# First FFN's down sums: copied from PSUM by ScalarE and added to the residual in DRAM by accumulating DMAs, in groups of up to four hidden tiles

## The chip, the cores and the metric

The kernel runs on one core of a Trainium2 chip. The metric is the time of one launch on the device, in microseconds (us). TensorE is called PE here, VectorE DVE, ScalarE ACT, GpSimd POOL, and SP is the engine that issues most of the DMAs.

## The reference, cut to what matters

One decoder layer on 1088 tokens (a prompt of 1024 and 8 x 8 sample tokens) of width 1024, in float32:

```python
def _swiglu(h, w_gate, w_up, w_down):
    return (jax.nn.silu(h @ w_gate) * (h @ w_up)) @ w_down
...
    x = x + 0.5 * _swiglu(_rmsnorm(x, ffn_a_norm), ffn_a_gate, ffn_a_up, ffn_a_down)
    h = _rmsnorm(x, mix_norm)
    q, k, v, u, g_attn, g_ssm = jnp.split(h @ w_in, SPLIT_POINTS, axis=-1)
...
    x = x + merged @ w_out
    x = x + 0.5 * _swiglu(_rmsnorm(x, ffn_b_norm), ffn_b_gate, ffn_b_up, ffn_b_down)
```

The change is in the product with `ffn_a_down` (hidden width 2816 = 22 tiles of 128) and its addition to `x`.

## The kernel before

Everything is held transposed: a tile has 128 channels on its partitions and up to 1088 tokens along its rows, so the residual `x` is eight tiles `xr0` to `xr7` (index `m`), and the FFN's hidden values are 22 tiles `hid0` to `hid21` (index `j`). The tokens are cut into three columns `c` of 384, 384 and 320. Float32 products are made of three matmuls each: weights and inputs are split into a high part (a rounded copy, by ACT, line 104) and a low part (the rest, by DVE, line 105), and `mm3` (line 113) multiplies high by high, high by low, and low by high.

The first FFN (phase `a`) first computes all hidden tiles and stores them in DRAM (`hd`). Then come the *down units* that the change touches, made by `d_unit`: each takes a group of two or three hidden tiles and, for each of the 24 pairs (m, c), runs 3 matmuls for each of its tiles into a PSUM tile `psda`, and line 817 on DVE adds half of the PSUM tile to `xr`. The groups are the list `cuts` in `ffn_units` (line 1885): tiles 0-1, 2-4, 5-7, 8-10, 11-13, 14-16, 17-18, 19-21. PSUM tiles come from two rings of three and two (`"ddada"`), so five are in use at most. The second FFN (phase `b`) has the same units with `psdb`.

The residual is read from DRAM (`xd`) when the first unit starts (`need_x`, line 1784) and stays in SBUF until the last unit, which goes through the columns one after the other and starts the next RMSNorm: squares on ACT, their sums over the channels by PE (line 499), a power on POOL (line 156), then the scaled tiles for the next projection (`psu`).

All tiles of this size come from one pool of 43 buffers (`NB`, tag `B`): weights, hidden tiles, their high and low parts, and `xr`. A tile that is given a used buffer waits until the one that held it is no longer read. `run_units` issues the loads of the next two groups when a unit starts. While a unit's matmuls are issued, each `yield` issues one step of the next unit's `prep` (the split of one hidden or weight tile: ACT, then DVE) and, by `tick`, one step of a *side program*. From the second unit (tile 2) on this is `ssm_setup`, which makes tables for the later state-space part: DVE operations on 128x512 tiles in 8 rounds, with two sets of PE transposes (`cT`, line 1072, and `vl`, line 1092), one set of PE matmuls (`k`, line 1100), ACT copies and sines, and stores of tables by POOL's DMAs. All instructions of an engine run in the order in which they are issued.

Of the kernel before, what the change touches and what calls it, by code (L numbers as in the profile page):

```python
# [7 lines left out]
F32 = mybir.dt.float32  # L8
F32R = mybir.dt.float32r
AF = mybir.ActivationFunctionType  # L10
OP = mybir.AluOpType
# [9 lines left out]
T = 1088  # L21
# [45 lines left out]
class Kern:  # L67
# [711 lines left out]
    def d_unit(s, ph, js, last=None):  # L779
        nc = s.nc  # L780
        stt = {}

        class U:
            st = stt

            def load(u):
                st = u.st
                for j in js:
                    r = s.B([128, D], f"rdown{ph}{j}", F32)
                    nc.sync.dma_start(r, s.a[f"ffn_{ph}_down"][0, j * 128:(j + 1) * 128, :])  # L790
                    st[j] = r
                    r = s.B([128, T], f"rhid{ph}{j}", F32)
                    nc.sync.dma_start(r, s.hd[j])
                    s.hid[j] = r
                if js[0] == 0:
                    s.need_x(0)

            def prep(u):
                st = u.st
                eng = s.nc.vector  # L800
                for j in js:
                    hi, lo = s.B([128, T], f"hidh{ph}{j}"), s.B([128, T], f"hidl{ph}{j}")
                    s.split(s.hid[j], hi, lo, eng)
                    s.hid[j] = hi, lo
                    yield
                    s.wsplit(st, j, [128, D], f"dn{ph}{j}", eng)
                    yield

            def one(u, m, c):
                st = u.st  # L810
                o, n = CH[c]
                u.n = getattr(u, "n", 0) + 1
                ps = s.bank("ddada"[u.n % 5], f"psd{ph}{js[0]}_{m}_{c}")
                yield from s.mm3(ps[:, :n], [(st[j][0][:, m * 128:(m + 1) * 128], st[j][1][:, m * 128:(m + 1) * 128],
                                              s.hid[j][0][:, o:o + n], s.hid[j][1][:, o:o + n]) for j in js])
                xs = s.need_x(m)[:, o:o + n]
                nc.vector.scalar_tensor_tensor(xs, ps[:, :n], 0.5, xs, op0=OP.mult, op1=OP.add)  # L817

            def main(u):
                if last is None:  # L820
                    order = [(0, 0), (0, 1), (1, 0), (1, 1), (0, 2), (1, 2)] + [(m, c) for m in range(2, KC) for c in range(3)]
                    for i, (m, c) in enumerate(order):
                        yield from u.one(m, c)
                        if i % 2:
                            yield
                    return
                for c in range(3):
                    for m in range(KC):
                        yield from u.one(m, c)
                        s.sq_add(c, m, last[0])  # L830
                        yield
                    s.sq_flush()
                    s.pending += s.norm_steps(c, *last)
        return U()
# [1047 lines left out]

    def ffn_units(s, ph, last):
        s.hid = {}
        cuts = (0, 2, 5, 8, 11, 14, 17, 19, 22)
        out = [s.g_stage(ph)]
        if ph == "b":
            out.insert(0, s.plain_unit(ph))
        js = [tuple(range(a, b)) for a, b in zip(cuts, cuts[1:])]
        out += [s.d_unit(ph, j) for j in js[:-1]]  # L1890
        out.append(s.d_unit(ph, js[-1], last) if last else s.last_unit(ph, js[-1]))
        return out
# [119 lines left out]
```

## Time and profile before

| | |
|---|---|
| median of 3 runs | 2351.44 us (2351.07 to 2352.85) |
| the profiled execution's own time | 2351.03 us |
| its span, from the first to the last instruction | 2349.3 us |
| PE busy | 2275.0 us (97%) |
| DVE busy | 1404.2 us (60%) |
| ACT busy | 853.0 us (36%) |
| POOL busy | 264.3 us (11%) |

The first FFN's down units run from 514.2 to about 831.8 us after the span's start, those of the second FFN from 2069.2 to about 2295 us. Shares over the whole span say little about either; the rows below are of these stretches.

### The profile page before, as it was taken

To read this page: it belongs to the slowest core of one execution; us is meant where nothing else is said; L and a number is where in the kernel's file an instruction comes from. 1 tells how busy PE (TensorE), PEld (TensorE's weight loads), DVE (VectorE), ACT (ScalarE), POOL (GpSimd) and SP (SyncE) were. 2 spreads that over 40 slices of the span, in tenths; PEclk is the share of its full clock that TensorE was granted. 3 is DMA by queue.
4 is the path that set the end of the run, shared out by engine and by line. 5 is a ranking of instruction groups with operands and counts; after the bars stand their busy time and mean duration, and the time that the engine had idled before them with its cause. 6 is when DMAs were issued, how large, how long until landed. Compare 5 with 4: busy or idle time off the path is not lost. (4 is left out here: it accounts for less than half of the span.)

```text
span 2349.3 us, 39687 instructions
## 1 busy us (share of the span) xinstructions
PE 2275.0 (97%) x15910; PEld 2216.6 (94%) x15910; DVE 1404.2 (60%) x2961; ACT 853.0 (36%) x1919; POOL 264.3 (11%) x427
## 2 busy tenths in 40 slices
PE   7999999999889999999999999999999999999998
PEld 6999999998878998999998999989999999999997
DVE  7655555568888742446775666457555555575555
ACT  5333333331221341236666653223333333322113
POOL 2000000014333140002221100000000000000000
PEclk9999999999999999999999999999999999999999
DMA  6222222273443237740224164203222222362202
GB/s 197 79 73 83 83 75 64 83 255 108 140 138 106 73 131 215 238 107 28 69 75 111 45 231 136 73 5 140 79 83 66 73 83 83 126 256 72 86 10 77
DMA packets 234104, 250.04 MB, mean 106 GB/s; under 512 B 35056, under 2 KB 197024, under 8 KB 233888
## 3 DMA queue, kind: packets, MB, share of 16 engines
q1 hardware_dynamic: 218208, 205.42, 28.2%
q0 software_dynamic: 14272, 39.79, 4.8%
q8 instruction: 125, 2.05, 0.4%
q10 hardware_dynamic: 1440, 2.31, 0.3%
q14 instruction: 59, 0.48, 0.1%
HBM read 176.93 MB, written 74.60 MB: 107 GB/s over the span
## 5 line engine op out<-in xcount | busy, mean ns | idle before, releaser
L817 DVE SCALAR_TENSOR_TENSOR xr<-psdb,xr 128x384 f32<-128x384 f32 x168 | 87.9, 534 | 93.2 <-PE psdb L113 92.9
L817 DVE SCALAR_TENSOR_TENSOR xr<-psda,xr 128x384 f32<-128x384 f32 (+1 forms) x192 | 100.7, 532 | 33.5 <-PE psda L113 33.1
L1534 POOL TENSOR_SCALAR sm<-sm,sum 128x256 f32<-128x256 f32 x128 | 59.9, 487 | 312.3 <-DVE sum L1532 202.9
L113 PE MATMUL Ya<-b21h,a12a 128*128 128x272 f32 x320 | 67.1, 290 | 0.0
L113 PE MATMUL Xa<-t4h,a22a 128*128 128x272 f32 x320 | 67.1, 290 | 0.0
L113 PE MATMUL Yb<-b21h,a12b 128*128 128x272 f32 x320 | 67.1, 290 | 0.0
L113 PE MATMUL Xb<-t4h,a22b 128*128 128x272 f32 x320 | 67.1, 290 | 0.0
L113 PE MATMUL Vb<-b22h,s4b 128*128 128x272 f32 x320 | 67.1, 290 | 0.0
L113 PE MATMUL Va<-b22h,s4a 128*128 128x272 f32 x320 | 67.1, 290 | 0.0
L732 POOL DMA_DIRECT2D hd<-hidb x40 | 21.6, 540 | 403.0 <-DVE hidb L730 403.0
L732 POOL DMA_DIRECT2D hd<-hida x40 | 21.6, 540 | 403.0 <-DVE hida L730 403.0
L1518 ACT ACTIVATE sm<-sm,nm 128x256 f32<-128x256 f32 x128 | 63.3, 503 | 2.0 <-DVE nm L1505 1.9
L113 PE MATMUL Xa<-t2h,s2a 128*128 128x272 f32 x320 | 63.8, 290 | 0.0
L113 PE MATMUL Va<-t1h,s1a 128*128 128x272 f32 x320 | 63.8, 290 | 0.0
L113 PE MATMUL Xa<-t3h,s3a 128*128 128x272 f32 x320 | 63.8, 290 | 0.0
L113 PE MATMUL Xb<-t2h,s2b 128*128 128x272 f32 x320 | 63.8, 290 | 0.0
L113 PE MATMUL Xb<-t3h,s3b 128*128 128x272 f32 x320 | 63.8, 290 | 0.0
L113 PE MATMUL Vb<-t1h,s1b 128*128 128x272 f32 x320 | 63.8, 290 | 0.0
L113 PE MATMUL Xb<-b11h,a11b 128*128 128x272 f32 x320 | 63.8, 290 | 0.0
L113 PE MATMUL Xa<-b11h,a11a 128*128 128x272 f32 x320 | 63.8, 290 | 0.0
L104 ACT ACTIVATE hidhb<-rhidb 128x1088 fp32r<-128x1088 f32 x22 | 24.3, 1103 | 89.7 <-PE psdb L113 65.1
L113 PEld LDWEIGHTS Ya<-b21h,a12a 128*128 128x128 f32 x320 | 52.7, 188 | 0.0
(1455 smaller groups left out, 8498.9 us busy)
## 6 DMA issues: line engine op xcount, KB each, us to landing
xr<-xd SPq DMA_DIRECT2D x24, 544.0 KB, 6.0
rhida<-hd SPq DMA_DIRECT2D x22, 544.0 KB, 5.2
rhidb<-hd SPq DMA_DIRECT2D x22, 544.0 KB, 5.2
rdowna<-in_ffn_a_down_dram SPq DMA_DIRECT2D x22, 512.0 KB, 3.9
rdownb<-in_ffn_b_down_dram SPq DMA_DIRECT2D x22, 512.0 KB, 4.8
hd<-hida POOLq DMA_DIRECT2D x40, 272.0 KB, 2.9
hd<-hidb POOLq DMA_DIRECT2D x40, 272.0 KB, 2.7
rgatea<-in_ffn_a_gate_dram SPq DMA_DIRECT2D x20, 512.0 KB, 3.9
```

What stands on the lines that cost most here:

```text
L104: s.nc.scalar.activation(hi, raw, AF.Copy)
L113: s.nc.tensor.matmul(ps, w, x, start=i == 0 and not more, stop=i == n - 1, skip_group_check=more)
L732: nc.gpsimd.dma_start(s.hd[j, :, o:o + HC], hid[j][:, o:o + HC])
L817: nc.vector.scalar_tensor_tensor(xs, ps[:, :n], 0.5, xs, op0=OP.mult, op1=OP.add)
L1518: A.activation(sm[:, h, :], sm[:, h, :], AF.Exp, bias=nm[:, h:h + 1], accum_out=sm4[:, h:h + 1])
L1534: s.nc.gpsimd.tensor_scalar(sm[:, h, :], sm[:, h, :], sm4[:, h:h + 1], 1.0, op0=OP.mult, op1=OP.mult)
```

## The change

In the first FFN's units but the last (`u.dram`), the residual is no longer loaded. ACT copies half of each PSUM tile into a new tile `dy` (line 821 of the changed kernel), and when a channel tile's third column is there, POOL issues a DMA that adds the `dy` tile to `xd` in DRAM (line 823). The last unit (tiles 19-21) is as before, but it is now the one that loads `xr`. The groups of phase `a` become 0-1, 2-4, 5-8, 9-12, 13-15, 16-18, 19-21: seven units instead of eight. Phase `b` keeps its groups.

```diff
         class U:
             st = stt
 
+            dram = ph == "a" and last is None
+
             def load(u):
...
-                if js[0] == 0:
+                if js[0] == 0 and not u.dram:
                     s.need_x(0)
...
+                if u.dram:
+                    if m not in u.y:
+                        u.y[m] = s.B([128, T], f"dy{js[0]}_{m}", F32)
+                    nc.scalar.activation(u.y[m][:, o:o + n], ps[:, :n], AF.Copy, scale=0.5)
+                    if c == 2:
+                        nc.gpsimd.dma_start(s.xd[m], u.y[m], accum_op=OP.add)
+                    return
                 xs = s.need_x(m)[:, o:o + n]
                 nc.vector.scalar_tensor_tensor(xs, ps[:, :n], 0.5, xs, op0=OP.mult, op1=OP.add)
 
             def main(u):
+                u.y = {}
...
-        cuts = (0, 2, 5, 8, 11, 14, 17, 19, 22)
+        cuts = (0, 2, 5, 9, 13, 16, 19, 22) if ph == "a" else (0, 2, 5, 8, 11, 14, 17, 19, 22)
```

The matmuls are the same in number, and PE's order differs only in where the side program's matmuls stand. Three places show what moves.

DVE while the unit of tile 5 runs. Before, the evictions (`xr<-psda`) stand between the splits of the next unit's tiles (`hidla`, `dna..l`) and the side program's operations (`ph`, `lo`, `kk`, `S`):

```order
L817 SCALAR_TENSOR_TENSOR xr0_5266<-psda5_0_1_6323,xr0_5266 128x384
L105 TENSOR_TENSOR hidla8_6337<-rhida8_5854,hidha8_6336 128x1088
L1132 TENSOR_TENSOR ph0_6292<-ph0_6292,kc0_6294 128x512
L1133 TENSOR_TENSOR lo0_6295<-lo0_6295,kk0_6293 128x512
L105 TENSOR_TENSOR dna8l_6352<-rdowna8_5852,dna8h_6351 128x1024
L1135 TENSOR_TENSOR ph0_6292<-ph0_6292,lo0_6295 128x512
L1136 TENSOR_SCALAR ph0_6292<-ph0_6292 128x512
L817 SCALAR_TENSOR_TENSOR xr1_5268<-psda5_1_0_6342,xr1_5268 128x384
L105 TENSOR_TENSOR hidla9_6369<-rhida9_5858,hidha9_6368 128x1088
```

In the changed kernel the same stretch of DVE holds splits and side operations alone:

```order
L105 TENSOR_TENSOR hidla9_6376<-rhida9_5858,hidha9_6375 128x1088
L1142 TENSOR_TENSOR ph0_6324<-ph0_6324,kc0_6326 128x512
L1143 TENSOR_TENSOR lo0_6327<-lo0_6327,kk0_6325 128x512
L105 TENSOR_TENSOR dna9l_6391<-rdowna9_5856,dna9h_6390 128x1024
L1145 TENSOR_TENSOR ph0_6324<-ph0_6324,lo0_6327 128x512
L1146 TENSOR_SCALAR ph0_6324<-ph0_6324 128x512
L105 TENSOR_TENSOR hidla10_6412<-rhida10_5862,hidha10_6411 128x1088
```

The evictions have left DVE; nothing else there has changed its place.

ACT in the same stretch, first before:

```order
L104 ACTIVATE dna8h_6351<-rdowna8_5852 128x1024
L104 ACTIVATE hidha9_6368<-rhida9_5858 128x1088
L1138 ACTIVATE kk0_6293<-ph0_6292 128x512
L1139 ACTIVATE kk0_6293<-kk0_6293 128x512
L1140 ACTIVATE ph0_6292<-ph0_6292,c1_68 128x512
L104 ACTIVATE dna9h_6377<-rdowna9_5856 128x1024
```

and in the changed kernel:

```order
L821 ACTIVATE dy5_1_6400<-psda5_1_0_6381 128x384
L104 ACTIVATE hidha10_6411<-rhida10_5862 128x1088
L1148 ACTIVATE kk0_6325<-ph0_6324 128x512
L1149 ACTIVATE kk0_6325<-kk0_6325 128x512
L1150 ACTIVATE ph0_6324<-ph0_6324,c1_68 128x512
L821 ACTIVATE dy5_1_6400<-psda5_1_1_6402 128x384
L104 ACTIVATE dna10h_6423<-rdowna10_5860 128x1024
```

The copies out of PSUM (line 821) now stand in ACT's queue, some of them behind the sine `kk<-ph` (line 1148; line 1138 before), which reads what DVE makes.

POOL at the end of the side program, just before the last unit. Before:

```order
L1143 DMA tab3_5555<-kk7_7869 128x4x128
L1144 DMA tab3_5555<-ph7_7868 128x4x128
L1147 DMA tab2_5554<-kpad_5556 16x32x128 x8
L156 TENSOR_TENSOR rstd_8366<-ms_8362,mhalf_79 128x3
```

and in the changed kernel:

```order
L823 DMA xd_84<-dy16_5_8102 128x1088
L1153 DMA tab3_5547<-kk7_8116 128x4x128
L1154 DMA tab3_5547<-ph7_8115 128x4x128
L823 DMA xd_84<-dy16_6_8151 128x1088
L1157 DMA tab2_5546<-kpad_5548 16x32x128 x8
L823 DMA xd_84<-dy16_7_8202 128x1088
L156 TENSOR_TENSOR rstd_8414<-ms_8410,mhalf_79 128x3
```

The last accumulating DMA, that of channel tile 7, stands behind the eight copies of `kpad` to the table, and the load of `xr7` for the last unit has to wait for it.

## Rows read from the trace of the kernel before

**Rows 1.** The page's first part: busy us (share of the span) and instructions.

```profile
span 2349.3 us, 39687 instructions
PE 2275.0 (97%) x15910; PEld 2216.6 (94%) x15910; DVE 1404.2 (60%) x2961; ACT 853.0 (36%) x1919; POOL 264.3 (11%) x427
```

**Rows 2.** Busy time by stretch: down units of phase a, then all with side program.

```profile
core 0: us, PE busy (x) PEld busy (x) DVE busy (x) ACT busy (x) POOL busy (x), PEclk, DMA share, GB/s
514.20:538.00 23.80, 23.80 (x146) 23.80 (x145) 19.09 (x31) 7.74 (x9) 16.65 (x31) 1.00 1.03 365
538.00:584.40 46.40, 41.64 (x234) 38.65 (x233) 39.62 (x132) 6.45 (x9) 15.62 (x8) 0.93 0.15 46
631.40:679.50 48.10, 42.74 (x246) 39.88 (x246) 40.68 (x73) 11.66 (x18) 18.07 (x28) 0.93 0.41 127
...
769.10:792.90 23.80, 23.80 (x146) 23.80 (x146) 18.80 (x30) 4.02 (x5) 5.85 (x10) 1.00 0.46 155
792.90:832.00 39.10, 38.06 (x236) 37.63 (x236) 30.32 (x60) 18.20 (x34) 10.44 (x10) 1.00 0.05 14
538.00:769.10 231.10, 207.81 (x1197) 195.98 (x1196) 198.07 (x415) 54.27 (x77) 80.28 (x107) 0.95 0.36 110
```

**Rows 3.** The same for three units of three tiles in phase b.

```profile
2093.00:2200.00 107.00, 107.00 (x651) 107.00 (x650) 57.90 (x90) 17.50 (x18) 0.00 (x0) 1.00 0.25 82
```

**Rows 4.** Who waited for whom, 514 to 832 us: total, times, longest.

```profile
ACT kk L1138 <- DVE ph L1136: 76.5, 7, 13.1
...
PE vl L1092 <- DVE S L1080: 12.7, 5, 5.5
...
PE psda L113 <- DVE xr L817: 7.7, 6, 2.6
...
PE k L1100 <- DVE C L1087: 2.9, 2, 2.2
```

**Rows 5.** PE by line, 537 to 832 us, the side program's matmuls: busy, mean ns.

```profile
L1100 PE MATMUL k<-C,S 128*16 128x128 f32 x64 | 10.3, 314 | 2.9 <-DVE C L1087 2.9
...
L1092 PE MATMUL vl<-c,S 128*128 128x128 f32 x32 | 6.3, 333 | 12.7 <-DVE S L1080 12.7
L1072 PE MATMUL cT<-c,ssmin 64*128 64x64 f32 x16 | 2.7, 247 | 0.0
```

**Rows 6.** DVE by line, 538 to 769 us: evictions, splits, one side operation.

```profile
L817 DVE SCALAR_TENSOR_TENSOR xr<-psda,xr 128x384 f32<-128x384 f32 (+1 forms) x120 | 63.3, 531 | 18.5 <-PE psda L113 18.3
L105 DVE TENSOR_TENSOR hidla<-rhida,hidha 128x1088 fp32r<-128x1088 f32 x14 | 18.0, 1283 | 0.0
...
L1126 DVE TENSOR_TENSOR kk<-ph,lo 128x512 f32<-128x512 f32 x8 | 5.5, 688 | 0.1
```

**Rows 7.** ACT by line, whole span: a copy of 128x384 out of PSUM.

```profile
L1403 ACT ACTIVATE ts<-pswgs 128x384 f32<-128x384 f32 x16 | 7.9, 492 | 21.9 <-PE pswgs L113 19.1 <-issue 2.8
```

**Rows 8.** DMA, 862 to 875 us, where stores of xr fill the queues.

```profile
q1 hardware_dynamic: 1972, 4.16, 91.4%
```

**Rows 9.** DMA issues on the page: KB each, us to landing.

```profile
xr<-xd SPq DMA_DIRECT2D x24, 544.0 KB, 6.0
...
hd<-hida POOLq DMA_DIRECT2D x40, 272.0 KB, 2.9
```

**Rows 10.** POOL in order of time, 768 to 776 and 514 to 600 us: start, us.

```profile
769.93 4.38 POOL L1147 DMA_DIRECT2D tab<-kpad  x7
775.07 0.64 POOL L1147 DMA_DIRECT2D tab<-kpad  x1 [0.75 <-DMA tab<-ph]
...
548.63 6.51 POOL L959 TENSOR_TENSOR prm<-prm 128x32 f32<-128x32 f32 x1 [2.21 <-DVE prm L956]
```

## Prediction, made before the changed kernel had run

> **What bounds the kernel now.** I read the first part of the page first: PE is busy in 97% of the span and no other engine in more than 60% [rows 1]. Over the whole kernel there is little to win, so the question is whether the changed stretch is one of the poor ones. The busy times by stretch say that it is [rows 2]. The unit of tiles 0-1 and that of tiles 17-18 run with PE busy throughout (23.80 of 23.80 us). Between them, from 538.0 to 769.1 us, five units of three tiles take 231.1 us; PE is busy in 207.8 of these, its granted clock is 0.95, and DVE is busy in 198.1 (86%). What differs there is the side program, whose DVE work shares the queue with the evictions.
>
> The control is phase b, where the same units run without a side program [rows 3]: three units in 107.0 us, or 35.67 each, with PE at 100%, clock 1.00, and the evictions still on DVE. Five units at that pace are 5 x 35.67 = 178.3 us, so the side program costs 231.1 - 178.3 = 52.8 us. Part of that is PE's own side work: its three groups are busy for 10.3 + 6.3 + 2.7 = 19.3 us [rows 5]. Matmuls overlap in the pipeline, so their net cost is less than that sum; half of it (about 10) is my lower end and 19.6 (the sum, rounded up) the upper; I take 15. This leaves 52.8 - 15, about 38 us (33 to 43), for waits and the loss of clock that goes with them.
>
> The waits name the places [rows 4]: PE waits 12.7 us in `vl` and 2.9 in `k` for DVE tables, and 7.7 in `psda`, where the eviction of an earlier PSUM tile (line 817) has not yet run. That is only 23.3 us of the 38; the rest I put down to matmuls at the lower clock (0.93 in the units shown) and to short gaps which that view does not group. The long waits of ACT (76.5 us in 7, for `ph` of DVE) cost nothing now, since nothing that PE needs soon stands behind them.
>
> **What goes.** In tiles 2 to 16 there are 120 evictions by DVE of 531 ns, 63.3 us in all [rows 6]. They all leave. DVE's work in this part falls from 198.1 to 134.8 us, 70% of the 193.3 us (178.3 + 15) that PE alone needs there. In the whole phase seven groups in place of eight make 168 evictions instead of 192, of which 144 are on ACT and the last unit's 24 stay on DVE.
>
> **What ACT gets.** The nearest row for a copy of 128x384 out of PSUM is 492 ns [rows 7], so the 144 copies are about 70 us (a little less, since every third is of 320). The part of tiles 2 to 16 gets some 115 of them, 56 us, on top of 54.3 [rows 2]: 110 of 193, or 57%. By load this is hidden. By order it may not be, which is a rival below.
>
> **The regrouping** changes no matmul. A group of four fills a PSUM tile in 1.98 us, one of three in 35.67 / 24 = 1.49. It costs nothing in itself; what it needs is buffers.
>
> **What POOL and the queues get.** 48 accumulating DMAs of 544 KB. Issue on POOL is bounded by its own rows: 0.64 us for one transfer of the `kpad` group, 4.38 for seven [rows 10], so 40 of them are some 25 us beside POOL's 80.3 in 231 [rows 2]; not a bound. On the queues, the stretch that is full of stores moved 4.16 MB at 91.4% of 13 us [rows 8], 11.9 us, so a plain 544 KB (0.557 MB) fills all 16 engines for 1.59 us. Tiles 2 to 18 have 40 of them: 64 us at that price. The queues' own work there is 0.36 x 231.1 + 0.46 x 23.8 = 94 us [rows 2], together 158 of some 225 us. So at the plain price the transfers are hidden.
>
> No row shows an accumulating DMA. Its lower bound is the plain 1.59 us; for the upper I go by 3 times that, 4.8 us, a read of the target and a write in place of one write with as much again lost to turning round (an estimate from that row, not a measurement). I take the plain price to twice it, in which the sum does not change: twice, 94 + 127 = 221, is just below 225.
>
> On this the Trainium skill has a rule that speaks against the change ("Collectives: The Full Stack", section "The bandwidth ceiling: the fold count and why AG ≠ RS ≠ AR"): a reducing transfer has two source reads for one write and so runs at about half the rate of a copy. No run here shows it yet. By the rule the sum would have 127 us of accumulates in place of 64, which is a rival below.
>
> **What is left of the 38 us.** Three costs stay or come.
>
> First, the bursts of DVE. At each `yield` DVE gets a split of 1.28 us and a side operation of about 0.69 [rows 6], while PE needs for the matmuls in between (eight of about 0.165 us, from 35.67 us for 216 matmuls) 1.3 us. DVE falls behind by up to some 5 to 8 us while the splits run and catches up in the other half of the unit. So PE's waits for `vl` and `k` do not all go: bounds 0 and 15.6 (12.7 + 2.9, [rows 4]); I take 6, under half, as the queue is shorter by the evictions.
>
> Second, the new `dy` tiles want used buffers, so an ACT copy may wait for an accumulate to land (in the order, the third `dy` tile of a unit takes the buffer of the second one, or of one two before). A plain store of 272 KB lands after 2.9 us and a load of 544 KB after 6.0 [rows 9]; I put an accumulate between 2.9 and 12. One `dy` tile is delayed also by the 6.51 us power on POOL, behind which its accumulate stands [rows 10]. Five PSUM tiles give PE 4 x 1.49 = 6 us to 4 x 1.98 = 7.9 us of slack. Most such waits lie within it: bounds 0 and 5, taken 2.
>
> Third, the last unit. It was PE-bound with a loaded `xr` (38.06 of 39.10, [rows 2]). Now `xr7` is loaded behind the last accumulate, and that stands on POOL behind eight copies of `kpad`, 4.38 + 0.64 = 5.0 us [rows 10]. Landing (6 to 12) and loading (6.0, [rows 9]) take 12 to 18 us. The first use of `xr7` comes eight groups later, 8 x 1.49 = 11.9 us, and PE is held only at the norm's sums that follow. Bounds 0 and 6; taken 2. The first unit, whose queues are full (1.03, [rows 2]), no longer has the eight loads of `xr`; as PE has no gap there, that gives nothing.
>
> **The sum.** 38 - 6 - 2 - 2 = 28 us. The profiled execution took 2351.03 us with a span of 2349.3, 0.4 us below the median of 2351.44, so the bases agree: 2351.0 - 28 = 2323 us. With the ends: 43 and no residual cost give 2308; 33 - 15.6 - 2 - 6 = 9 gives 2342.
>
> **The rivals.** *A, twice the price.* The 221 us of DMA would fit on average, but the side program's stores are bunched (0.15 of the queues in one unit, 0.41 in another, [rows 2]). At the density of 91.4% [rows 8] 221 us become 242, 17 more than 225; with good luck none. Half of it, 8 us: 2331 us. For it speaks that the add must read its target; against it that reads and writes may overlap.
>
> *B, ACT in PSUM's way.* The copies stand behind `kk<-ph`, for which ACT waits 76.5 us in 7 waits, 10.9 each, longest 13.1 [rows 4]. Behind these PE has 7.9 us of slack in a unit of four tiles. If DVE stays as late as now, each of eight rounds costs PE 10.9 - 7.9 = 3 us, 24 in all, and the gain is 28 - 24 = 4: 2347 us. Against it: without the evictions DVE reaches `ph` sooner, by the 63.3 us spread over eight rounds, 8 us each.
>
> *C, the other side.* The accumulates bound the stretch. They must then take so long that the queues need the whole 254.9 us (231.1 + 23.8) of before, less the 2 at the end: (252.9 - 94) / 40 = 4.0 us each, 2.5 times the plain price, or 2.2 times at a density of 91.4%. From there on ACT waits for buffers, PE for ACT, and the kernel is slower. At three times it is 94 + 191 = 285 us, 312 at that density; the middle, 299, is 44 above 254.9 and with 2 for the end gives 2397 us. For it speaks that `dy` waits chain directly into ACT's queue; against it, that a plain load of 544 KB lands in 6.0 us although many share the queues [rows 9], so that an add would have to cost far more than its read.
>
> **How the numbers follow.** Forecast .64 (its own range 2308 to 2342), A .14, B .12, C .10. The predicted time is the forecast's, 2323. The range of 8 in 10 is 2311 to 2342: it holds the forecast but for its lowest tail, and A; what is left out is C (.10), the larger part of B (.07) and tails (.03). A change of 0.2%, 4.7 us, is about what a measurement of this kernel can tell from none. Slower by more than that: C, .10. Within it: half of B, .06. Faster: the forecast, A and the other half of B, .84.
>
> **What would show it.** In the changed trace the stretch of tiles 2 to 18 should take some 225 us in place of 255, with DVE near 70%, ACT near 57% and PE's clock near 1.00. `psda` should wait for ACT in place of DVE, by a few us in all; `vl` and `k` for DVE by half of now. An accumulate's share of the queues should be near 0.7 in that stretch; if it is near 0.9 or above and ACT's longest waits are for buffers that a DMA frees, A or C is right. If ACT's waits for `ph` stay near 11 us and PE waits for the copies behind them, B is. The wait at the last unit for `xr7` should be below 6 us. I would be wrong by most if an accumulate has a latency far above 12 us, since then every reuse of a `dy` buffer stops ACT and so PE, though the queues are not full.

## The result, and the profile after

The changed kernel is slower: 2372.18 us (median of 4 runs, 2371.33 to 2373.76) against 2351.28 of the kernel before; ratio 1.0088, interval 1.0071 to 1.0106. I had forecast 2323 us, 28 us faster; it is 21 us slower, outside the range of 2311 to 2342. Of my cases, the one on the other side (C, chance .10) had the right sign, but not the right way to it.

From the page of the changed kernel, its first part, two lines of the part on DMA (queue: packets, MB, share of 16 engines) and the line of the accumulates (count, KB each, median us to landing); they answer to [rows 1, 8, 9]:

```profile
span 2370.6 us, 39777 instructions
PE 2279.5 (96%) x15910; PEld 2221.8 (94%) x15910; DVE 1329.7 (56%) x2793; ACT 913.0 (39%) x2063; POOL 308.4 (13%) x475
...
q0 software_dynamic: 21184, 66.53, 11.1%
...
HBM read 176.93 MB, written 101.34 MB: 117 GB/s over the span
...
xd<-dy POOLq DMA_DIRECT2D x48, 544.0 KB, 7.8
```

The same lines on POOL's queue in the kernel before:

```profile
q0 software_dynamic: 14272, 39.79, 4.8%
...
HBM read 176.93 MB, written 74.60 MB: 107 GB/s over the span
```

DVE lost 74.5 us of work (1404.2 to 1329.7), as it should. POOL's queue grew from 4.8% of 2349.3 us to 11.1% of 2370.6, by 263.1 - 112.8 = 150.3 us: 3.13 us of all 16 engines for each of the 48 accumulates, twice the plain 1.59 of [rows 8]. The bytes written grew by their 26.7 MB; the bytes read did not change, so if an add reads its target, this count does not show it; the share of the queues does show the longer time.

Where did the time go? The busy times by stretch, one row for each unit from tile 2 on, then the units of tiles 2 to 18 together (compare [rows 2]):

```profile
core 0: us, PE busy (x) PEld busy (x) DVE busy (x) ACT busy (x) POOL busy (x), PEclk, DMA share, GB/s
537.30:600.90 63.60, 45.19 (x234) 42.91 (x234) 33.68 (x113) 19.44 (x35) 26.93 (x20) 0.81 0.94 222
600.90:659.40 58.50, 53.16 (x317) 51.08 (x317) 32.92 (x51) 24.93 (x44) 25.99 (x37) 0.97 0.77 174
659.40:712.60 53.20, 51.94 (x318) 49.98 (x317) 28.66 (x45) 22.93 (x42) 26.23 (x37) 1.00 0.91 228
712.60:757.30 44.70, 41.40 (x237) 39.27 (x236) 31.33 (x50) 21.04 (x42) 25.50 (x36) 0.92 0.88 209
757.30:801.10 43.80, 40.59 (x241) 38.90 (x240) 26.68 (x42) 19.80 (x38) 14.64 (x19) 0.96 0.98 236
801.10:853.00 51.90, 41.07 (x237) 40.33 (x236) 30.34 (x60) 20.07 (x40) 18.79 (x22) 0.87 0.45 128
537.30:801.10 263.80, 232.28 (x1339) 222.13 (x1339) 153.26 (x300) 108.14 (x199) 119.28 (x148) 0.93 0.89 213
```

Two rows stand out: the unit of tiles 2-4 takes 63.6 us (46.4 before) and the last one 51.9 (39.1 before). In each PE is idle a long time, and its granted clock is lower (0.81 and 0.87). The middle units have queues as full (0.77 to 0.98) and lose little: a full queue alone does not stop PE here.

The waits in the unit of tiles 2-4 (total, times, longest; compare [rows 4]):

```profile
engine line waited for: us in total, times, longest us
DVE hidla L105 <- ACT dy L821: 20.7, 1, 20.7
...
PE psda L113 <- ACT dy L821: 14.8, 2, 10.2
...
ACT hidha L104 <- DMA xd<-dy: 14.5, 1, 14.5
```

PE waits for a copy by ACT, but it is not the copy that is slow: ACT itself stands for 14.5 us before the *split* of the next unit's first hidden tile (`hidha5`; the views leave numbers out), until an accumulate lands. In time, POOL first, then its eight accumulates as a group (first and last issue; shortest, median and longest time to landing), then SP, ACT and DVE (start, duration, idle time before and what ended it):

```profile
531.35 4.07 POOL L943 DMA_DIRECT2D kpad<-zero  x8 [0.29 <-POOL zero L941]
535.41 7.13 POOL L823 DMA_DIRECT2D xd<-dy  x8
539.85 8.19 POOL L960 TENSOR_TENSOR prm<-prm 128x32 f32<-128x32 f32 x1
...
L823 POOL DMA_DIRECT2D xd<-dy x8: 983/2078/3263, 535.4 to 539.3; - x8
...
DMA to landing us min/median/max: 5.6/16.7/29.9
...
511.02 0.33 SPq L795 DMA_DIRECT2D rhida<-hd  x1
541.09 0.33 SPq L792 DMA_DIRECT2D rdowna<-in_ffn_a_down_dram  x1
...
541.06 0.49 ACT L821 ACTIVATE dy<-psda 128x384 f32<-128x384 f32 x1 [1.07 <-PE psda L113]
556.10 1.11 ACT L104 ACTIVATE hidha<-rhida 128x1088 fp32r<-128x1088 f32 x1 [14.55 <-DMA xd<-dy]
...
569.25 1.06 ACT L104 ACTIVATE dna7h<-rdowna 128x1024 fp32r<-128x1024 f32 x1 [7.07 <-issue]
...
560.16 1.29 DVE L105 TENSOR_TENSOR hidla<-rhida,hidha 128x1088 fp32r<-128x1088 f32 x1 [20.70 <-ACT dy L821]
```

The first `dy` tile was full at 519 us. But POOL was issuing the side program's opening transfers (from 515.9 to 535.4 us): the side program's first step is issued ahead of the unit of tiles 0-1, only the rest runs from tile 2 on. So the eight accumulates of tiles 0-1 left together, from 535.4 to 539.3 us: 25 us of queue time (8 x 3.13) at once. They land one after the other, the first at 541.0 us (5.6 after its issue), the last at 569.2 (29.9 after). The buffers of their `dy` tiles go, by the order of the pool, to four loads of SP (the first leaves at 541.09) and to `hidha5`, `hidla5`, `hidla7` and `dna7h` of the next unit: not to other `dy` tiles, but to splits that stand at the head of ACT's and DVE's queues. The trace fits this to a tenth of a microsecond where it can be read best: the fifth, sixth and eighth accumulate land at 556.1, 560.1 and 569.2, and the splits of `hidha5`, `hidla5` and `dna7h` start at 556.10, 560.16 and 569.25. (DVE's wait is put down to a copy by ACT that had long been done, and ACT's second one, of 7.07 us, to no releaser.) Behind the held split on ACT stand the copies, and behind these the five PSUM tiles and PE. PE stands twice, for 10.6 us until 558.6 and for 4.9 us until 570.7, and both ends follow such a split.

In the last unit (POOL, then SP, then DVE, then PE's wait by the view of waits):

```profile
803.41 0.95 POOL L823 DMA_DIRECT2D xd<-dy  x1
803.98 4.09 POOL L1157 DMA_DIRECT2D tab<-kpad  x6
808.90 0.63 POOL L1157 DMA_DIRECT2D tab<-kpad  x1 [0.82 <-DMA tab<-ph]
812.24 0.63 POOL L1157 DMA_DIRECT2D tab<-kpad  x1 [2.71 <-DMA xd<-dy]
813.38 0.91 POOL L823 DMA_DIRECT2D xd<-dy  x1 [0.51 <-ACT sqtf L481]
...
822.63 0.32 SPq L1794 DMA_DIRECT2D xr<-xd  x1
...
819.50 0.56 DVE L826 SCALAR_TENSOR_TENSOR xr<-psda,xr 128x384 f32<-128x384 f32 x1 [6.29 <-DMA xr<-xd]
826.46 0.56 DVE L826 SCALAR_TENSOR_TENSOR xr<-psda,xr 128x384 f32<-128x384 f32 x1 [5.93 <-DMA xr<-xd]
...
PE sspf L499 <- DVE sqsumf L488: 9.8, 1, 9.8
```

The accumulate of channel tile 7 was issued at 813.4 us, 10 us after that of tile 6; `xr7`'s load was issued at 822.6, and DVE had it at 826.5. PE stood before the norm's sums, for 10.1 us from start to start of its matmuls (9.8 in the view of waits). About half of those 10 us between two accumulates is the issue of eight copies; the rest comes from the program as it is built. POOL's DMAs use eight semaphores in turn, and each waits until the transfer eight places before it has landed. The seventh copy of `kpad` waits so for the table's `ph`, the eighth for the accumulate of tile 6 (landed at 811.95), and the accumulate of tile 7 for the first copy (812.83).

### The profile page after: what moved, and what is told of

Same layout as the page of the kernel before. It is cut to its first block, busy times and chain, and to the rows that moved or that the text cites. A ratio compares the mean times of both kernels' runs of the same rounds, so it can differ in the third digit from the quotient of the medians.

```text
span 2370.6 us, 39777 instructions
## 1 busy us (share of the span) xinstructions
PE 2279.5 (96%) x15910; PEld 2221.8 (94%) x15910; DVE 1329.7 (56%) x2793; ACT 913.0 (39%) x2063; POOL 308.4 (13%) x475
## 3 DMA queue, kind: packets, MB, share of 16 engines
q0 software_dynamic: 21184, 66.53, 11.1%
## 5 line engine op out<-in xcount | busy, mean ns | idle before, releaser
L821 ACT ACTIVATE dy<-psda 128x384 f32<-128x384 f32 x144 | 65.6, 472 | 84.4 <-PE psda L113 75.4
L729 ACT ACTIVATE ua<-ua 128x272 f32<-128x272 f32 x40 | 17.3, 432 | 93.7 <-DVE ua L728 93.7
```

What stands on the lines that cost most here:

```text
L729: A.activation(d["u"], d["u"], AF.Silu)
L821: nc.scalar.activation(u.y[m][:, o:o + n], ps[:, :n], AF.Copy, scale=0.5)
```

## The experiments

Theory 1: an accumulate costs the queues twice a plain transfer, and that matters where something waits for one to land, at the two ends. Theory 2: the copies in ACT's queue hold PSUM, whatever the DMAs cost. Others are named where they come. Each run went beside runs of the kernel before (2352.0 to 2352.4 us). The unit lengths below, from the first `psda` matmul of a unit to that of the next (of the last unit, to the next projection), are of the profiled runs, in us; the unit of tiles 0-1 took 23.8 in all of these.

| kernel | 2-4 | 5-8 | 9-12 | 13-15 | 16-18 | 19-21 | median |
|---|---|---|---|---|---|---|---|
| changed | 63.6 | 58.5 | 53.2 | 44.7 | 43.8 | 51.7 | 2372.2 |
| plain stores | 50.0 | 56.6 | 53.2 | 43.9 | 42.5 | 45.6 | 2347.6 |
| no DMAs | 43.2 | 56.6 | 53.2 | 43.9 | 42.5 | 38.8 | 2338.5 |
| plain in the middle | 62.7 | 56.7 | 53.2 | 45.7 | 44.0 | 50.0 | 2367.1 |
| plain at the ends | 50.6 | 60.0 | 53.2 | 44.0 | 42.5 | 45.4 | 2353.1 |
| `kpad` after | 62.9 | 61.0 | 53.2 | 43.8 | 42.5 | 46.0 | 2367.1 |
| opening later | 53.2 | 64.3 | 53.2 | 43.7 | 44.1 | 47.5 | 2366.9 |
| both | 53.3 | 63.9 | 53.2 | 43.8 | 42.5 | 46.2 | 2359.7 |

**Plain stores.**

```diff
-nc.gpsimd.dma_start(s.xd[m], u.y[m], accum_op=OP.add)
+nc.gpsimd.dma_start(s.xd[m], u.y[m])
```

> The 48 DMAs write dy over the residual in DRAM instead of adding to it; the addition is left out, all else stays. Theory 1 (an accumulate takes about 3.1 us of all 16 queues, twice a plain transfer, and so frees dy buffers and xr7 too late): the time on POOL's DMA queue falls by some 70 us, the stall of the unit of tiles 2-4 (10.6 and 4.9 us) and that at the norm's sum in the last unit (10.1 us) shrink to about half, and the time is near 2355 us. Theory 2 (the copies stand in ACT's queue in the way of PSUM, whatever the DMA costs): within 4 us of the changed kernel, 2372.

Measured: 2347.55 us, ratio to before 0.9982 (0.9973 to 0.9991). Its page:

```profile
q0 software_dynamic: 21184, 66.53, 8.0%
...
xd<-dy POOLq DMA_DIRECT2D x48, 544.0 KB, 4.2
```

The same packets and bytes take 8.0% of 2344.5 us, 187.6; less 112.8 that is 1.56 us for a transfer. So the add itself costs 24.6 us of the kernel's time (2372.18 to 2347.55), more than I had expected. PE's two stops in the unit of tiles 2-4 fall from 15.5 to 2.9 us, that in the last unit from 10.1 to 4.4: theory 1.

**No DMAs.** The two lines with the DMA go.

> The 48 accumulating DMAs are left out, so the sums of tiles 0 to 18 are lost; the copies by ACT, the groups and the loads of xr in the last unit stay. Theory 1 (the transfers are what costs): both long stalls go, with the low clock behind them, and the stretch comes down to what I had forecast, 2325 to 2335 us. Theory 2 (ACT's queue): only the last unit's wait goes, 12 us, 2360 us, and PE still waits for copies in the units of tiles 5 to 18.

Measured: 2338.51 us, 0.9946 (0.9931 to 0.9961): 14 us better than before. The end of both long stalls is theory 1's, and 9.0 us of the plain stores' time goes too; but the time is not what I had forecast for free transfers. The two units of tiles 13 to 18 each still hold PE for 3.5 us before `psda`, and here theory 2 is right on a small scale. ACT and DVE in the unit of tiles 13-15:

```profile
699.48 0.45 ACT L821 ACTIVATE dy<-psda 128x320 f32<-128x320 f32 x1
706.83 0.63 ACT L1146 ACTIVATE kk<-ph 128x512 f32<-128x512 f32 x1 [6.90 <-issue]
...
708.63 0.47 ACT L821 ACTIVATE dy<-psda 128x384 f32<-128x384 f32 x1
...
706.32 0.43 DVE L1144 TENSOR_SCALAR ph<-ph 128x512 f32<-128x512 f32 x1
```

The sine waits until 706.83 us for DVE's `ph` (done 706.75), and the copies stand behind it: my rival B.

**Groups of before.** The changed kernel with the eight groups, 56 accumulates.

> The changed kernel with the eight groups of before (56 accumulates). Theory 1: eight more accumulates are 25 us more on queues that are nearly full, 2375 to 2390 us. Theory 2, in the form that the groups of four tiles leave too few free buffers: faster than the changed kernel, about 2360 us.

Measured: 2374.58 us, 1.0099 (1.0082 to 1.0116). The groups of four are not the cause of the loss as a whole: with the old ones, and eight accumulates more, the time is 2.4 us higher. They do bear on the first stall: with the old groups the unit of tiles 2-4 takes 53.9 us in place of 63.6, and the later units take that back. The new groups alone, with evictions by DVE, were not tried. By a count of tiles, two groups of four that are split (32), the raw tiles of a third (8) and `xr` (8) are more than the 43 buffers.

**Which accumulates cost?** Plain stores for the middle units, and for the first and the last before the end:

```diff
-nc.gpsimd.dma_start(s.xd[m], u.y[m], accum_op=OP.add)
+nc.gpsimd.dma_start(s.xd[m], u.y[m], **({} if js[0] in (5, 9, 13) else dict(accum_op=OP.add)))
...
+nc.gpsimd.dma_start(s.xd[m], u.y[m], **({} if js[0] in (0, 16) else dict(accum_op=OP.add)))
```

> The changed kernel with plain stores in the units of tiles 5-8, 9-12 and 13-15 (24 of 48; the addition is left out there). If the accumulates cost time at the two ends alone (what waits for the first unit's, and for the last unit's), the time stays within 5 us of the changed kernel, 2367 to 2372. If their use of the queues as a whole sets the time, half of the 24.6 us that the plain stores won come back: 2360 us.

> The changed kernel with plain stores in the units of tiles 0-1 and 16-18 (16 of 48; the addition is left out there). If the ends are what costs, nearly the whole 24.6 us come back: 2348 to 2354 us. If use of the queues sets the time, a third of it: 2364 us.

Measured: 2367.11 us (24 plain in the middle, 5 us back) and 2353.11 us (16 plain at the ends, 19 us back). Together that is 24.1 of the 24.6 of all 48; the eight accumulates of the unit of tiles 2-4 add in both runs. Use of the queues as a whole would have given 12 and 8. The ends are what costs.

**Order on POOL.** First, the eight copies of `kpad` after the last accumulate:

```diff
+for _ in range(6):
+    yield
 for r in range(8):
     nc.gpsimd.dma_start(s.tab2[:, r * 16 ...
```

> The changed kernel with the side program's last eight copies of kpad issued six steps later, so that the last accumulate stands ahead of them on POOL. If the last unit's 10.1 us wait comes from the order on POOL (the last accumulate was issued 10 us after the one before it), the wait falls to about 5 us and the time to 2366 to 2368 us. If the DMA queues are so full that the order of issue makes no difference, 2372 us.

Measured: 2367.07 us, 1.0061 (1.0044 to 1.0078), PE's stop 4.7 us. As expected of the order. Second, 17 instructions of the side program's opening later:

```diff
 load_part(0)
-load_part(1)
-z = s.sm([16, 512], "zero")
-nc.gpsimd.memset(z, 0.0)
-for q in range(8):
-    nc.gpsimd.dma_start(kpad[:, 4 * q:4 * q + 4, 0:128], z...
 yield
...
+zeros(6)
+load_part(1)
 cmul(ER, EI, ...
```

> The changed kernel with 17 POOL instructions of the side program's start (the second set of ssmin loads, the zeros and their eight copies to kpad) moved about a unit later, so that the accumulates of tiles 0-1 are issued as their dy tiles are ready, from about 519 us in place of 535. If lateness on POOL makes the stall of the unit of tiles 2-4, its 63.6 us come down to about 50 and the time to 2357 to 2362 us. If the price of eight accumulates on the queues (25 us) makes it, the unit keeps most of its length and the time is above 2367 us.

Measured: 2366.88 us (2360.77 to 2369.14; the profiled run, from which the unit lengths are, is the fastest of the four, by 5.7 us), 1.0059 (1.0044 to 1.0074), above what lateness alone should give. POOL's accumulates of tiles 0-1 in it, and the split of `dna7h` on ACT:

```profile
522.72 4.52 POOL L823 DMA_DIRECT2D xd<-dy  x5
...
L823 POOL DMA_DIRECT2D xd<-dy x8: 852/967/1932, 522.7 to 534.7; - x8
...
DMA to landing us min/median/max: 5.4/15.6/20.4
...
555.21 1.06 ACT L104 ACTIVATE dna7h<-rdowna 128x1024 fp32r<-128x1024 f32 x1 [6.11 <-issue]
```

The accumulates leave from 522.7 us on, and the unit of tiles 2-4 falls by 10.4 us, as expected of the order (to 53.2; 50 was named). The rest of its stall is the price: the eight still land one after the other, the last at 555.1 us, 20.4 after its issue; the split of `dna7h` starts at 555.21, and PE, which has stood for 6.0 us, goes on at 556.6. The next unit grows by 5.8 us. Both moves together:

> Both moves together, with all 48 accumulates. If the whole loss is order on POOL at the two ends, the gains add: 2350 to 2356 us, level with the kernel before, and above the 2338.5 of the run without DMAs by the accumulates' price alone. If the transfers are what bounds, 2365 us or more.

Measured: 2359.68 us, 1.0033 (1.002 to 1.0046). The gains add (5.1 and 5.3 alone, 12.5 together, within the spread), but to less than expected: still 7.5 us slower than before, between the two cases that were named. The eighth accumulate lands at 557.6 us and `dna7h` starts at 557.70; PE has stood for 6.4 us by then. The same pair of times, within 0.1 us of each other, stands in every run of the table that has transfers, plain stores too (553.9 and 553.98). A run that gives the `dy` tiles buffers of their own was not made. Why the unit of tiles 5-8 takes 63.9 us there instead of 58.5 was not settled; PE's waits for `vl` and `k` in it are 2 us longer and its granted clock is 0.89.

**The adds on POOL, in SBUF.** The kernel before with `xr` kept, for all columns and (with `c == 2` in the condition too) for the third alone:

```diff
+if ph == "a" and last is None:
+    y = s.t(f"ev{js[0]}_{m}_{c}")[:, :n]
+    nc.scalar.activation(y, ps[:, :n], AF.Copy, scale=0.5)
+    nc.gpsimd.tensor_tensor(xs, xs, y, op=OP.add)
+    return
 nc.vector.scalar_tensor_tensor(xs, ps[:, :n], 0.5, xs, ...
```

> The kernel before, with xr kept in SBUF and the groups of before; ACT copies half of each PSUM tile to a small tile (six of them rotate) and POOL adds it to xr there. No DMA is added. If POOL has the room (24 adds a unit of 0.7 to 1.5 us in 46 us, an estimate from its 487 ns on 128x256), the units shorten as in the run without DMAs and the time is 2335 to 2343 us. If the adds stand on POOL behind its waits for DVE (up to 12.9 us each), the six tiles run out, ACT stops and PE with it, and the time is above 2365 us.

> The same for the third column alone: 56 of the 168 evictions by ACT and POOL, the others by DVE as before. If DVE's load sets the waits of before in proportion, a third of the 14 us that the run without DMAs won, 2346 to 2348 us; if POOL's waits stop ACT, they stop it here too, but the six tiles last three times as long: 2352 or more.

Measured: 2449.34 us (1.041, 1.0394 to 1.0427) and 2369.68 us (1.0078, 1.0063 to 1.0093); both worse, the second well above the 2352 from which its worse case began. From the first, POOL by line and the waits, 514 to 940 us:

```profile
L820 POOL TENSOR_TENSOR xr<-xr,ev 128x384 f32<-128x384 f32 x168 | 182.0, 1110 | 23.0 <-ACT ev L819 22.1
...
ACT ev L819 <- POOL xr L820: 47.8, 36, 16.8
...
PE psda L113 <- ACT ev L819: 44.6, 10, 13.7
```

An add takes 1.11 us, within my bounds, and ACT does run out of small tiles. The rest is in the last section.

**Groups of four a unit later, and the sines later.** Both moves on POOL with cuts at 0, 2, 5, 8, 12, 16, 19; then two `yield`s ahead of the first sine, in place of one after each of two other steps.

> Both moves on POOL, and the groups 0-1, 2-4, 5-7, 8-11, 12-15, 16-18, 19-21: the groups of four come one unit later, so that the first unit's dy buffers are not wanted at once by four-tile loads. All 48 accumulates add. If the first loss is buffers wanted before the accumulates land, the unit of tiles 2-4 falls from 53.3 to about 48 us and the next one loses less: 2348 to 2354 us, level with the kernel before. If the groups make no difference, 2358 to 2361 us as with both moves alone.

> The same, with the side program's sines on ACT issued two steps later (two other steps are joined, so that it ends where it did). If the copies that stand on ACT behind the sine, waiting for DVE's ph, are what holds PE in psda in the units of tiles 12 to 18 (two waits of 3.5 us there), these waits go: 4 to 8 us below the run without this. If DVE's lateness only shows elsewhere (in vl and k), no difference, within 3 us.

Measured: 2363.98 us (1.0051, 1.0038 to 1.0065) and 2360.47 us (1.0039, 1.0026 to 1.0051). With the later fours, the unit of tiles 2-4 does fall to 46.9 us, but the next two (of three and of four tiles) take 57.9 and 60.6: the lateness moves on. With the sines later, the waits in question go, and others grow. PE's waits, 514 to 850 us, without and with:

```profile
PE psda L113 <- ACT dy L821: 16.3, 4, 8.8
...
PE vl L1107 <- DVE S L1095: 13.4, 3, 7.0
```

```profile
PE vl L1106 <- DVE S L1094: 24.7, 4, 13.2
PE psda L113 <- ACT dy L821: 4.4, 2, 4.0
```

The 16.3 us before `psda` fall to 4.4, and `vl` waits 11.3 us more. The units of tiles 2 to 18 together lose 2.8 us (261.7 to 264.5 in the profiles), and what is gained is in the last unit (39.9 in place of 46.8), where `xr7` has landed 16.3 us after the unit's start in place of 20.7. So one wait goes and another comes. How much of it is DVE's own lateness is not shown: in the longest wait of `vl` (13.2 us) DVE itself stands for 5.07 us before the split of `hidla10`, whose buffer is that of a `dy` tile which lands just then. No version here beats the kernel before with the sums intact.

## Why the prediction was wrong

The starts of PE's matmuls split the stretch of tiles 2 to 18 into parts, in us. The 1224 matmuls of `psda` at their median distance (174 ns for 384 columns, 147 for 320) make 202.0 in each kernel; a distance over 0.6 us counts as a wait, and the extra time of shorter ones as low clock where less than 0.9 of it was granted. The line between waits and low clock is good to about 1 us.

| kernel | stretch | side work | waits in `psda` | waits in `vl`, `k`, `cT` | low clock | short gaps |
|---|---|---|---|---|---|---|
| before | 254.8 | 16.1 | 9.4 | 17.0 | 6.2 | 4.2 |
| no DMAs | 239.4 | 14.0 | 6.7 | 9.3 | 3.3 | 4.1 |
| changed | 263.9 | 14.8 | 22.9 | 11.4 | 9.1 | 3.7 |

**What bounds it** was right: side work 16 us (I took 15), everything else 36.8 (38). (The 115 copies that I put in tiles 2 to 16 are 104 by the groups; nothing rests on them.)

**The price of an accumulate** was within my bounds (1.59 to 4.8 us): 3.13. By the rule of the Trainium skill that I had weighed ("Collectives: The Full Stack", section "The bandwidth ceiling: the fold count and why AG ≠ RS ≠ AR", on the two source reads of a ring's reduce) it is twice a copy; the trace agrees, 3.13 to 1.56. The failure is the sentence behind it, "in which the sum does not change". I compared totals over 225 us, where 221 fit. The adds cost 24.6 us all the same, since eight came at once at the start and the last ones had a reader waiting. Rival A had the price right and took 8 us for it, and rival C set its break-even at 2.2 to 2.5 times; both made the same error: they asked when the queues fill, not when something waits. My own sign of A or C did show: the queues were at 0.89 from tile 2 to 18, and ACT's longest wait (14.5 us) was for a buffer that an accumulate freed.

**The second cost, buffers (bounds 0 and 5, taken 2)** is the largest failure. Against the run without DMAs, the unit of tiles 2-4 lost 20.4 us and the other middle units 1.9 + 0.0 + 0.8 + 1.3 = 4.0. The landing was mis-sized with it: I put it between 2.9 and 12 us, and in the burst of eight it took up to 29.9 (median of all 48: 7.8). I looked at `dy` tiles that wait for other `dy` tiles, in the middle, where PSUM's slack does cover them. I did not follow who takes the buffers of the first unit, and dismissed that unit because its PE has no gap. The rows that I had were enough: POOL is busy for 16.65 of that unit's 23.8 us with the opening transfers [rows 2], which stand before the accumulates in the order, and the splits use the same pool.

**The third, the last unit (bounds 0 and 6, taken 2)**: 51.7 - 38.8 = 12.9 us. The chain was the right one, eight `kpad` copies and then landing and load, and these two took 9.2 and 3.9 us, together 13.1, within the 12 to 18 named. What was mis-sized is the issue: the accumulate of tile 7 left 12.3 us after the unit's start in place of about 5, as the copies took 8.9 us, with waits of 0.8 and 2.7 us for transfers eight places before. PE ran on for 17.0 us, 5 more than the first use of `xr7` that I had named, and still stood for 10.1. Putting the copies behind won 5 us.

**The first, DVE's bursts (taken 6)**: the waits in `vl` and `k` were 9.3 us without the DMAs. Rival B came on top of it, not in its place, at 6.7 us in `psda`; and the low clock and short gaps (10.4 before, 7.4 here) I had counted among what goes. These are the terms by which free transfers win 14 us instead of the 32 that my sum had ahead of the two DMA costs.

## What to carry to other kernels

A transfer that is cheap on average is dear where something waits for it: look at the first and the last of a series, and follow each buffer that it holds to the next owner, and that owner's place in its queue. For work moved to an engine that also issues DMAs, list what stands ahead of the first transfer and of the last one. Where a late engine is the cause of waits, taking instructions from it returns only part of them: here, in the run without DMAs, the evictions' leaving took PE's waits for DVE's tables from 17.0 to 9.3 us, and the copies that now stand behind DVE's results brought 6.7 us.

## What the hardware showed beside this

A DVE operation of the same shape slows down while POOL adds in SBUF. DVE's splits of 128x1088 from 538 to 760 us, with a third of the adds on POOL and then with all (1283 ns before, [rows 6]):

```profile
L105 DVE TENSOR_TENSOR hidla<-rhida,hidha 128x1088 fp32r<-128x1088 f32 x14 | 21.3, 1523 | 0.0
```

```profile
L105 DVE TENSOR_TENSOR hidla<-rhida,hidha 128x1088 fp32r<-128x1088 f32 x14 | 27.2, 1945 | 13.2 <-ACT hidha L104 13.2
```

They take 19% and 52% longer, and relief by POOL is none here: with a third of the adds there, DVE has 48 evictions less in tiles 2 to 18 and is yet busy for 226.1 us in place of 216.9 (198.07 + 18.80, [rows 2]; columns as in the busy times by stretch):

```profile
537.20:808.20 271.00, 232.39 (x1341) 220.69 (x1339) 226.10 (x397) 78.79 (x131) 146.07 (x171) 0.94 0.35 109
```

The Trainium skill has a rule for the slower splits ("SBUF — State Buffer", section "Who interferes with whom": a DVE instruction with two SBUF inputs contends with one of POOL that reads SBUF), and the trace agrees.

POOL's wait before the eighth copy of `kpad`, 2.71 us at 812.24 us above, looks like one of the hardware and is the program's: it is for the semaphore of the transfer eight places before.
